# Issuing the fourth and fifth image pairs' loads from another place in a dilated 3x3 convolution

## The chip, the cores and the metric

The kernel runs on one core of a Trainium2 chip. A core has a matrix engine (TensorE, PE in the profile), a vector engine (VectorE, DVE), a scalar engine (ScalarE, ACT), GpSimd (POOL), a synchronisation engine (SyncE, SP) that here only issues transfers, and 16 DMA engines that move data between the device memory (HBM) and the on-chip memory (SBUF). TensorE writes its results to a separate accumulator memory (PSUM). The metric is the device time of one execution in microseconds; 13 executions of the kernel before have a median of 128.17 us, from 127.54 to 131.16.

## The reference

A 3x3 convolution with dilation 2 and zero padding 2, in float32: 16 images of 64 channels, 64 x 64 pixels, to 128 channels.

```python
batch, c_in, h, w, c_out, k, dilation = 16, 64, 64, 64, 128, 3, 2
...
x_pad = np.pad(x, ((0, 0), (0, 0), (pad, pad), (pad, pad)), mode='constant')
...
                    output[b, co] += weight[co, ci, kh, kw] * x_pad[b, ci, kh*dilation:kh*dilation+h, kw*dilation:kw*dilation+w]
```

The input is 16.8 MB, the output 33.6 MB, the weights 0.3 MB.

## The kernel before

**Tiling.** Two images share the 128 partitions: one pair's input is a tile of 128 partitions (two images times 64 channels) by 4096 pixels in float32, 2 MB, and there are 8 pairs. Each pair is worked off in four groups of 16 rows, so the main loop (L196) runs over 32 groups, G = 0 to 31. One pair's output is 128 channels by 2 x 4096 pixels, 4 MB.

**What a group does.** The rows are paired two apart, so that part of the products is shared: VectorE adds row blocks (`rowsum`, L85, into `xs`), TensorE forms the shared product psP from `xs` and two further products psA and psB from the casted input (all matmuls are at L174), ScalarE copies psP from PSUM to SBUF (`p_sb`, L230), and VectorE adds it to psA and to psB into the output tile `osb` (L237). There is only one PSUM buffer for psP (`ppool`, bufs=1), so the next group's psP waits for the copy.

**Input.** `load` (L61) fetches one pair's float32 input into one of three buffers (`fpool`, bufs=3). ScalarE casts it to float16 in four chunks per pair (`cast`, L73); casts are numbered c = 0 to 31. `casts(G)` (L153) is called in each group behind the copy of psP (in group 0 ahead of it) and runs up to two casts, up to seven casts ahead of the group for the first two pairs, up to three ahead later. When a pair's last cast has been issued, that pair's float32 buffer is free, and the same function issues the load of the pair three later into it (L162).

**Queues.** SyncE issues the weights (L88), the first pair's load in two pieces (L89) and the second and third pair's loads (L90, L91), and after that only stores (L188). All later loads (fourth to eighth pair) are issued by ScalarE, between its casts and copies. Every transfer is split over the same 16 DMA engines; in the profile q1 holds what SyncE issued and q10 what ScalarE issued. The stores of a pair, one per image, are issued when its fourth group is done (L253, L254); the last pair's are cut into smaller pieces.

**Order.** The schedule is written by hand: each engine runs its instructions in the order of the program, and waits where data isn't there.

Of the kernel before, what the change touches and what calls it, by code (L numbers as in the profile page):

```python
# [10 lines left out]
def kernel(  # L11
# [7 lines left out]
    nc = tc.nc  # L19

    B, CI, H, W = x.shape
# [15 lines left out]
    NG = H // GR  # L37
# [5 lines left out]
    XF = 3  # L43
# [17 lines left out]
    def load(pb, cuts=(0, H), queue=nc.sync):  # L61
        x32_tiles[pb] = fpool.tile([P, HW], f32, tag="x32", name="x32")
        for lo, hi in zip(cuts[:-1], cuts[1:]):
            queue.dma_start(  # L64
                out=x32_tiles[pb][:, lo * W : hi * W], in_=x_pair[pb, :, lo * W : hi * W]
            )

    def cast(c):
        pb, g = divmod(c, NG)
        lo, hi = chunk_rows[g]  # L70
        if g == 0:
            x16_tiles[pb] = xpool.tile([P, HW], f16, tag="x16", name="x16")
        nc.scalar.copy(  # L73
            out=x16_tiles[pb][:, lo * W : hi * W], in_=x32_tiles[pb][:, lo * W : hi * W]
        )

    def rowsum(c):
        pb, g = divmod(c, NG)
        if g == 0:
            xs_tiles[pb] = sxpool.tile([P, HW // 2], f16, tag="xs", name="xs")  # L80
        v = x16_tiles[pb][:, g * GR * W : (g + 1) * GR * W].rearrange(
            "p (b e q) -> p b e q", e=2, q=2 * W
        )
        s = xs_tiles[pb][:, g * NH : (g + 1) * NH].rearrange("p (b q) -> p b q", q=2 * W)
        nc.vector.tensor_tensor(out=s, in0=v[:, :, 0], in1=v[:, :, 1], op=add)  # L85
# [67 lines left out]
    def casts(G):  # L153
        for n in range(2 if G else 3):
            c = ahead[0]
            if c >= ngroups or c > G + (7 if c < 2 * NG else 3):
                return
            cast(c)
            ahead[0] += 1
            if c % NG == NG - 1 and c // NG + XF < npairs:  # L160
                k = c // NG + XF
                load(k, (0, H) if k < 6 else (0, H // 2, H), queue=nc.scalar)  # L162

    def product(ps, src, kind, blk0, nblk, first, last):
        for j in (1, 0, 2):
            dw = (j - 1) * d
            o0, o1 = max(0, -dw), W - max(0, dw)
            t = kind * KW + j
            for hb in range(2):
                pp = slice(hb * CI, (hb + 1) * CI)  # L170
                rhs = src(pp, dw + o0, dw + o1)
                po = ps[:, hb * NH + blk0 * 2 * W : hb * NH + (blk0 + nblk) * 2 * W]
                po = po.rearrange("p (r w) -> p r w", w=W)[:, :, o0:o1]
                nc.tensor.matmul(  # L174
                    out=po,
                    lhsT=w_sb[pp, t * CO : (t + 1) * CO],
                    rhs=rhs,
                    start=first and j == 1,
                    stop=last and j == 2,
                )  # L180

    def blocks(x16, b0, n, e):
        v = x16.rearrange("p (b e r w) -> p b e r w", e=2, r=2, w=W)
        return lambda pp, c0, c1: v[pp, b0 : b0 + n, e, :, c0:c1]

    def store(pb, m, r0=0, r1=H, rows=((0, P),)):
        for lo, hi in rows:
            nc.sync.dma_start(  # L188
                out=out_img[2 * pb + m, lo:hi, r0 * W : r1 * W],
                in_=o_tiles[pb][lo:hi, m * HW + r0 * W : m * HW + r1 * W],  # L190
            )
# [4 lines left out]
    for G in range(ngroups):  # L196
        pb, g = divmod(G, NG)
        x16 = x16_tiles[pb]
        xs = xs_tiles[pb].rearrange("p (r w) -> p r w", w=W)
        if g == 0:  # L200
            o_tiles[pb] = opool.tile([P, 2 * HW], f32, tag="osb", name="osb")
        o = o_tiles[pb].rearrange("p (m b e q) -> p m b e q", m=2, e=2, q=2 * W)
        b0 = g * NBLK

        def summed():
            ps = ppool.tile([P, 2 * NH], f32, tag="p", name="psP")
            sv = lambda pp, c0, c1: xs[pp, g * GR // 2 : (g + 1) * GR // 2, c0:c1]
            product(ps, sv, 0, 0, NBLK, True, True)
            return ps

        if G:
            psP = summed()

        psA = apool.tile([P, 2 * NH], f32, tag="ab", name="psA")
        product(psA, blocks(x16, b0, NBLK, 1), 1, 0, NBLK, True, False)
        z = 1 if g == 0 else 0
        product(psA, blocks(x16, b0 + z - 1, NBLK - z, 1), 2, z, NBLK - z, False, True)

        psB = apool.tile([P, 2 * NH], f32, tag="ab", name="psB")
        product(psB, blocks(x16, b0, NBLK, 0), 3, 0, NBLK, True, False)  # L220
        z = 1 if g == NG - 1 else 0
        product(psB, blocks(x16, b0 + 1, NBLK - z, 0), 4, 0, NBLK - z, False, True)

        if not G:
            psP = summed()

        if not G:
            casts(0)
        p_sb = spool.tile([P, 2 * NH], f32, tag="psb", name="p_sb")
        nc.scalar.copy(out=p_sb, in_=psP)  # L230
        if G:
            casts(G)
        if G + 1 < ngroups:
            rowsum(G + 1)
        pv = p_sb.rearrange("p (m b q) -> p m b q", m=2, q=2 * W)
        for e, ps in ((0, psA), (1, psB)):
            nc.vector.tensor_tensor(  # L237
                out=o[:, :, b0 : b0 + NBLK, e],
                in0=ps.rearrange("p (m b q) -> p m b q", m=2, q=2 * W),
                in1=pv,  # L240
                op=add,
            )

        if pb == npairs - 1:
            if g % 2 == 1:
                store(pb, 0, (g - 1) * GR, (g + 1) * GR)
                if g == NG - 1:
                    store(pb, 1, (g - 1) * GR, H - ROWS4)
                    store(pb, 1, H - ROWS4, H, FOUR)
                else:  # L250
                    store(pb, 1, (g - 1) * GR, (g + 1) * GR)
        elif g == NG - 1:
            store(pb, 0)  # L253
            store(pb, 1)  # L254
# [37 lines left out]
```

## Time and profile before

| | us |
|---|---|
| median of 13 runs | 128.17 |
| lowest and highest run | 127.54, 131.16 |
| the profiled execution | 127.58 |
| its span, from the first to the last instruction | 125.7 |
| PE busy, share of the span | 104.7 (83%) |
| DVE busy, share of the span | 90.8 (72%) |
| ACT busy, share of the span | 65.0 (52%) |
| bytes moved by DMA, mean rate | 50.78 MB, 404 GB/s |
| issue of the fourth, fifth and sixth pairs' loads | 10.88, 19.21, 36.87 |
| issue of the first pair's stores | 23.28 and 23.67 |

The profile's page gives busy time by engine, then the span in 40 equal slices of 3.14 us (a digit is the busy share in tenths, 9 meaning 90% or more), then groups of instructions, and a chain of waits followed back from the last instruction. Other views of the same trace give the chain in order of time, a table of chosen stretches, the timeline of one engine, and the DMA queues in a stretch. All times are counted from the first instruction. Names like `psP` or `x` stand for all buffers of that name; "ACTq" and "SPq" are the two engines' instructions that issue transfers.

### The profile page before, as it was taken

How to read it: one execution, taken by the hardware profiler on the slowest of the kernel's cores; microseconds unless marked ns; L12 is line 12 of the kernel's file. 1: busy time of each engine (PE TensorE's matmuls, PEld its weight loads, DVE VectorE, ACT ScalarE, POOL GpSimd, SP SyncE). 2: the span in 40 equal slices, each digit the busy share in tenths (PEclk: the TensorE clock that was granted, in tenths of full speed). 3: DMA queues.
4: the chain of work that ended last, by engine and by line, in shares of the span. 5: the costliest groups of instructions: out<-in, count | busy, mean ns of one | idle time of the engine just before them, and what ended most of it. 6: DMA issues, size and time to landing. Idle time of an engine off the chain costs nothing.

```text
span 125.7 us, 2335 instructions
## 1 busy us (share of the span) xinstructions
PE 104.7 (83%) x1000; PEld 56.7 (45%) x1000; DVE 90.8 (72%) x103; ACT 65.0 (52%) x68; POOL 2.2 (2%) x8
## 2 busy tenths in 40 slices
PE   6884999999999999999999999999999999500000
PEld 2351555555555555555555555555555555200000
DVE  0660998988898889798969898889888988700000
ACT  4377794366656665666566666666666633100000
POOL 2400000000000000000000000000000000000000
PEclk9999999999999999999999999999999999965555
DMA  4999999999999999999999999999999999999971
GB/s 109 391 434 448 438 427 422 427 302 433 427 433 433 427 417 433 417 443 417 409 448 407 433 433 417 433 420 427 433 448 422 427 417 427 427 417 427 424 325 54
DMA packets 4466, 50.78 MB, mean 404 GB/s; under 512 B 488, under 2 KB 488, under 8 KB 1000
## 3 DMA queue, kind: packets, MB, share of 16 engines
q1 hardware_dynamic: 3448, 40.14, 75.7%
q10 hardware_dynamic: 1008, 10.49, 20.5%
q8 instruction: 8, 0.13, 0.4%
q14 instruction: 2, 0.02, 0.0%
HBM read 17.07 MB, written 33.55 MB: 403 GB/s over the span
## 4 chain that ended last, share of the span: by engine, by line
PE 76%; DMA 6%; ACT 2%; issue 1%; DVE 1%; DVEq 1%; SPq 1%; ACTq 0%
PE psA L174 30%; PE psB L174 29%; PE psP L174 16%; DMA x<-in_x_dram 6%; DVE osb L237 1%; DVEq L287 1%; ACT p_sb L230 1%; ACT x L73 1%; SPq L64 0%; SPq L88 0%; ACTq L64 0%; DVEq L237 0%
## 5 line engine op out<-in xcount | busy, mean ns | idle before, releaser
L174 PEld LDWEIGHTS <-w_sb 64*128 64x128 f16 x960 | 54.6, 94 | 46.8 <-issue 2.1
L230 ACT COPY p_sb<-psP 128x1024 f32<-128x1024 f32 x32 | 32.4, 1012 | 37.5 <-PE psP L174 18.0
L237 DVE TENSOR_TENSOR osb<-psA,p_sb 128x1024 f32<-128x1024 f32 x32 | 39.2, 1225 | 14.2 <-PE psA L174 8.4
L174 PE MATMUL psA<-x,w_sb 64*128 64x496 f16 (+3 forms) x384 | 45.1, 365 | 0.3 <-ACT x L146 0.3
L174 PE MATMUL psB<-x,w_sb 64*128 64x496 f16 (+3 forms) x384 | 45.1, 365 | 0.0
L237 DVE TENSOR_TENSOR osb<-psB,p_sb 128x1024 f32<-128x1024 f32 x32 | 39.1, 1221 | 0.0
L73 ACT CAST x<-x 128x1024 f16<-128x1024 f32 (+2 forms) x31 | 32.1, 1044 | 0.4 <-DMA x<-in_x_dram 0.4
L174 PE MATMUL psP<-xs,w_sb 64*128 64x496 f16 (+1 forms) x192 | 26.0, 371 | 1.8 <-ACT p_sb L230 1.8
L85 DVE TENSOR_TENSOR xs<-x 128x512 f16<-128x512 f16 x32 | 13.3, 416 | 0.7 <-ACT x L73 0.7
L101 PE MATMUL dm<-zero 128*128 128x512 f16 x10 | 4.1, 532 | 1.2 <-DVE zero L93 1.2
L111 DVE CAST wd<-w 128x192 f16<-128x192 f32 x1 | 0.5, 505 | 2.7 <-DMA w<-in_weight_dram 2.7
L101 PEld LDWEIGHTS <-zero 128*128 128x128 f16 x10 | 1.0, 120 | 2.6 <-issue 1.3
L124 PE MATMUL wt<-ident,wd 128*64 128x128 f16 x30 | 1.6, 241 | 0.5 <-DVE wd L111 0.5
L124 PEld LDWEIGHTS <-wd 128*64 128x64 f16 x30 | 1.0, 118 | 2.0 <-DVE wd L111 1.4
L113 ACT ACT_TABLE_LOAD x1 | 1.3, 1283 | 0.7 <-PEq L273 0.7
L113 ACT CAST wd<-w 128x192 f16<-128x192 f32 x1 | 0.5, 542 | 1.8 <-DMA w<-in_weight_dram 1.8
L136 ACT CAST w_sb<-wt 128x384 f16<-128x384 f32 x1 | 0.5, 478 | 1.4 <-PE wt L124 1.4
L93 DVE MEMSET zero<- 128x256 uint32 x1 | 0.3, 272 | 0.9 <-PEq L273 0.9
L138 DVE CAST w_sb<-wt 128x384 f16<-128x384 f32 x1 | 0.6, 558 | 0.4 <-PE wt L124 0.4
L112 POOL TENSOR_TENSOR wd<-w 128x192 f16<-128x192 f32 x1 | 0.8, 797 | 2.6 <-DMA w<-in_weight_dram 2.6
L146 ACT CAST x<-x 128x512 f16<-128x512 f32 x1 | 0.6, 618 | 0.4 <-DMA x<-in_x_dram 0.4
L115 POOL CAST wd<-w 128x192 f16<-128x192 f32 x1 | 0.8, 807 | 0.0
(11 smaller groups left out, 3.8 us busy)
## 6 DMA issues: line engine op xcount, KB each, us to landing
out_dram<-osb SPq DMA_DIRECT2D x14, 2048.0 KB, 17.3
x<-in_x_dram ACTq DMA_DIRECT2D x3, 2048.0 KB, 14.6
x<-in_x_dram SPq DMA_DIRECT2D x2, 2048.0 KB, 16.6
x<-in_x_dram ACTq DMA_DIRECT2D x4, 1024.0 KB, 15.6
out_dram<-osb SPq DMA_DIRECT2D x3, 1024.0 KB, 14.2
x<-in_x_dram SPq DMA_DIRECT2D x1, 1088.0 KB, 5.5
x<-in_x_dram SPq DMA_DIRECT2D x1, 960.0 KB, 7.3
out_dram<-osb SPq DMA_DIRECT2D x1, 704.0 KB, 14.1
```

Source lines behind the costliest of these rows:

```text
L73: nc.scalar.copy(out=x16_tiles[pb][:, lo * W : hi * W], in_=x32_tiles[pb][:, lo * W : hi * W])
L85: nc.vector.tensor_tensor(out=s, in0=v[:, :, 0], in1=v[:, :, 1], op=add)
L101: nc.tensor.matmul(out=dm[:, 0:512], lhsT=zero[:, 0:P], rhs=zero)
L112: nc.gpsimd.tensor_tensor(out=wdv[:, 3], in0=wv[:, 0], in1=wv[:, 1], op=sub)
L113: nc.scalar.copy(out=wdv[:, 2], in_=wv[:, 0])
L115: nc.gpsimd.tensor_copy(out=wdv[:, 4], in_=wv[:, 2])
L124: nc.tensor.matmul(out=wts[k % 3][r * CI : (r + 1) * CI, c0 + j * CO : c0 + (j + 1) * CO], lhsT=wd[:, t * CI : (t + 1) * CI], rhs=ident,)
L138: nc.vector.tensor_copy(out=t2[0], in_=t2[1])
L174: nc.tensor.matmul(out=po, lhsT=w_sb[pp, t * CO : (t + 1) * CO], rhs=rhs, start=first and j == 1, stop=last and j == 2,)
L230: nc.scalar.copy(out=p_sb, in_=psP)
L237: nc.vector.tensor_tensor(out=o[:, :, b0 : b0 + NBLK, e], in0=ps.rearrange("p (m b q) -> p m b q", m=2, q=2 * W), in1=pv, op=add,)
L287: with _tile.TileContext(nc) as tc:
```

## The change

The fourth pair's load (k = 3) stays at the same place in the program, after the last cast of the first pair in group 0, but is issued by SyncE (the default of `load`) in place of ScalarE. So it stands in SyncE's order between the third pair's load and the first pair's stores. The fifth pair's load (k = 4) is no longer issued after the last cast of the second pair, which is in group 2, but by ScalarE in group 6, after that group's cast. The later loads stay where they were.

```diff
@@ -159,7 +159,10 @@
             ahead[0] += 1
             if c % NG == NG - 1 and c // NG + XF < npairs:
                 k = c // NG + XF
-                load(k, (0, H) if k < 6 else (0, H // 2, H), queue=nc.scalar)
+                if k == XF:
+                    load(k)
+                elif k > XF + 1:
+                    load(k, (0, H) if k < 6 else (0, H // 2, H), queue=nc.scalar)
@@ -230,6 +233,8 @@
         nc.scalar.copy(out=p_sb, in_=psP)
         if G:
             casts(G)
+        if G == NG + 2:
+            load(XF + 1, queue=nc.scalar)
         if G + 1 < ngroups:
             rowsum(G + 1)
```

## The prediction

> **What bounds the kernel now.** I read the page first: the totals and the 40 slices.
>
> ```profile
> span 125.7 us, 2335 instructions
> PE 104.7 (83%) x1000; PEld 56.7 (45%) x1000; DVE 90.8 (72%) x103; ACT 65.0 (52%) x68; POOL 2.2 (2%) x8
> ...
> PE   6884999999999999999999999999999999500000
> ...
> DMA  4999999999999999999999999999999999999971
> GB/s 109 391 434 448 438 427 422 427 302 433 427 433 433 427 417 433 417 443 417 409 448 407 433 433 417 433 420 427 433 448 422 427 417 427 427 417 427 424 325 54
> ```
>
> TensorE is full from slice 5 on, but it stops some 15 us before the end, while the DMA row stays at 9 to the 38th slice. So the DMA engines are the bound, and TensorE is a second resource not far below it. The rate is flat at about 430 GB/s except at the start, at the end and in the ninth slice (25.1 to 28.3 us), where it is 302 although the engines are counted as busy.
>
> The second view is the chain of waits in order of time, for the start and the end.
>
> ```profile
> 9.92 0.94 ACT x L73
> 10.86 0.02 issue
> 10.88 0.38 ACTq L64
> 11.26 0.04 issue
> 11.30 1.02 ACT p_sb L230
> 12.33 0.04 issue
> 12.37 0.81 PE psP L174 x6
> ...
> 107.49 1.23 DVE osb L237
> 108.71 1.13 DVEq L287
> ```
>
> The chain follows compute alone: ScalarE's last cast of pair 0, the issue of the fourth pair's load, the first copy of psP, then TensorE without a break. That chain ends at 109.8; behind it only transfers run. The table by stretches and the timeline of SyncE's queue show it (engine columns, then granted clock, DMA share and GB/s):
>
> ```profile
> 0.00:1.70 1.70, 0.51 (x2) 0.24 (x3) 0.27 (x1) 0.97 (x1) 0.70 (x6) 1.00 0.00 0
> 0.00:23.00 23.00, 19.19 (x173) 9.60 (x175) 14.38 (x20) 14.38 (x17) 2.25 (x8) 1.00 0.94 383
> 1.70:5.00 3.30, 2.85 (x13) 0.90 (x12) 1.18 (x3) 0.86 (x2) 1.13 (x2) 1.00 0.97 311
> 25.00:28.20 3.20, 3.20 (x34) 1.74 (x32) 2.78 (x4) 2.06 (x2) 0.00 (x0) 1.00 0.98 307
> 83.00:96.00 13.00, 13.00 (x132) 7.24 (x128) 11.60 (x13) 8.23 (x9) 0.00 (x0) 1.00 1.01 429
> 109.90:120.00 10.10, 0.00 (x0) 0.00 (x0) 0.00 (x0) 0.00 (x0) 0.00 (x0) 0.54 1.00 423
> ```
>
> ```profile
> 0.74 0.40 SPq L88 DMA_DIRECT2D w<-in_weight_dram  x1
> ...
> 23.28 0.82 SPq L188 DMA_DIRECT2D out_dram<-osb  x2
> ...
> 109.87 3.55 SPq L188 DMA_DIRECT2D out_dram<-osb  x4
> ```
>
> After the last add 423 GB/s flow for another 10.1 us, about 4.3 MB of stores that had piled up. A later TensorE costs nothing as long as it is less than some 10 us later; every microsecond in which the DMA engines stand still before 120 us is paid in full. Undisturbed rate: 429 GB/s (row 83 to 96).
>
> The low slice belongs to the first store. Its issue is at 23.28; the DMA view from 23.3 to 26.8 shows what moved since:
>
> ```profile
> q10 hardware_dynamic: 82, 1.33, 104.3%
> q1 hardware_dynamic: 1, 0.00, 0.0%
> ```
>
> q1 is SyncE's queue (stores), q10 ScalarE's (here the fifth pair's load). For 3.5 us the store moves no row; only load rows pass, and from 25 us on more slowly. The stretch 25.0 to 28.2 moves 307 instead of 429: (429 - 307) / 429 x 3.2 = 0.91 us of DMA time is lost. That is what the change can win at most.
>
> **The change part by part.**
>
> *What is removed from ScalarE's start.* The issue of the fourth pair's load costs 0.38 us plus 0.04 (11.30 - 10.88 = 0.42) on the chain ahead of the first copy of psP. SyncE issues it now, behind the third pair's load; SyncE then waits for the last cast of pair 0 (10.86), and behind that wait only the first store is queued, which isn't due before 22.9. So TensorE, the adds and the first store come 0.42 earlier: the store is issued at 23.28 - 0.42 = 22.86. At the end this is worth nothing, because the 10 us backlog of stores hides it; without that backlog it would be a gain of 0.42.
>
> *The fourth pair's load in SyncE's queue.* Same 2 MB, same engines, now behind the third pair's load instead of beside it. Its data is first needed by the cast in group 9, at 38.9; cost 0. The second and third pairs' data come sooner, which nothing waits for (TensorE has no gap there).
>
> *The fifth pair's load moved.* It was issued at 19.21; now it follows the cast of group 6, which ends at 30.76, so about 30.4 with the shift. Its 0.34 us on ScalarE fits into the idle time before the next copy (1.22 us there; without that it would delay one copy by 0.34, hidden again by the backlog). Its data is needed by the cast at 51.8; even behind 4 MB of stores and shared with the sixth pair's load it lands by about 45. The sixth pair's load stays at 36.87 and queues behind it; it is needed at about 64. Cost 0 on the compute side.
>
> *What this does to the DMA engines.* This is the sum. Weights and four pairs are 288 + 1088 + 960 + 3 x 2048 KB = 8.68 MB. By 23.0 us the engines had been given 383 x 23.0 = 8.81 MB; a row of 16 KB is booked when it starts and 16 engines are on average half way through theirs (0.13 MB), so 8.68 MB are done at 23.0. In the old kernel the fifth pair's load is queued behind them. In the new one there is nothing, until the first store flows. How long does a DMA take from its issue to its first bytes on idle engines? The trace has one: the weights, issued at 0.74, no bytes before 1.70, bytes in the next 0.2 us, so 1.05 us. First store bytes at 22.86 + 1.05 = 23.91. Gap: 23.91 - 23.0 = 0.91 us, on all engines but a late one. Bounds: 0 (if the loads drain up to a microsecond later than the mean) and 22.86 + 3.5 - 23.0 = 3.4 (if the store takes the 3.5 us that it takes today behind full queues). I take 0.91, since the queue is empty then and the weights' row is the one for an empty queue.
>
> *What the first store itself costs.* The 0.91 us lost from 25.0 to 28.2 are no longer lost on loads. Whether the store still pays them on itself no row shows directly. Bounds: 0 (it was the mixing with loads) and 0.91 (it is the start of a store). The nearest row is the other start from an empty queue, that of the loads: 1.70 to 5.00 moves 311, (429 - 311) / 429 x 3.3 = 0.91 us lost with no store about. And mixing alone is not slow later: from slice 14 on loads and stores share the engines at about 425. So I take the full 0.91.
>
> Sum: gap +0.91, old loss -0.91, new loss +0.91: +0.91 us. Next stretch: pair 0's stores (4.2 MB, 9.8 us) then last from 23.9 to about 34.6; the fifth pair's load is queued from 30.4, the second pair's stores from 35.2, so no second gap. From there each pair brings 6.3 MB, 14.7 us of DMA, against 12.4 us of TensorE: saturated again to the end.
>
> Weighed against the Trainium skill: its page "DMA: Bandwidth & Descriptors", section "Latency and other measured facts", gives about 600 ns to the first byte for queues of this kind, where the trace has 1.05; by the page the gap would be 0.46 and the sum an estimated +0.46, no change that can be told. The same page, "Back-pressure in remote DMA", says that stalled writes hold up the other queues of their engine; it speaks of traffic between cores, and no run here shows the mechanism. It speaks against the change: the store's stall would remain when the loads are gone, and the sum would be the +0.91.
>
> The profiled execution took 127.58 (span 125.7 and 1.9 around it), the median of the runs is 128.17, 0.59 above. New profiled execution: 128.49; new median: 129.08, so 129.1.
>
> **The rivals.** (B) *No change:* the first store runs at full rate once it is alone, and its gap eats the gain: +0.91 - 0.91 = 0, 128.2. For it: the low stretch ends as soon as store rows flow. Against it: the slow start of the loads with nothing beside them.
>
> (C) *Faster:* no gap and no slow start. It decides if the engines still hold load rows when the store's first bytes are ready, that is, if the four loads end 0.9 us later than 23.0 or the store starts 0.9 earlier. Sum -0.91: 127.3. For it: the issue is at 22.86, before the drain, and the engines don't all drain at once. Against it: 1.05 us is the only latency on idle engines in the trace, and ending the loads later costs as much as it fills.
>
> (D) *Much slower:* the store needs 3.5 us from issue to bytes even on idle engines. Gap 3.4, sum +2.5 to +3.4: 130.6 to 131.5. For it: both transfers that I can see start that late (the fourth pair's load, issued at 10.88, too moves nothing until 14.3). Against it: engines were full in both cases, and the weights took 1.05.
>
> That the change doesn't do what it says is unlikely: SyncE and ScalarE each carry the load in the place named, and neither waits for anything late there. What can fail is "empty load queue" as a benefit, which is case B or A.
>
> **How the numbers follow.** A (slower by 0.91 and its bounds of 0.4 to 1.4) 0.47; B 0.32; C 0.16; D 0.05. A measurement of this kernel can tell about 0.5% (0.64 us) from no change: below 127.53 is faster, above 128.81 slower. Of A 0.38 lies above and 0.09 within; of B 0.28 within and 0.02 on either side; of C 0.15 below and 0.01 within; D is slower. Faster 0.17, same 0.38, slower 0.45. Range 127.4 to 130.2: it takes in A and B and reaches into C; left out are a good half of C and D. A's own range is 128.5 to 129.6.
>
> **What would show it.** In the new profile: a slice at about 23 us with the DMA share well below 9 (the gap, 0.9 us); q1 rows from about 23.9; the rate from 24 to 27 below 429 by about 0.9 us of DMA time (A) or not (B); no dip at 25 to 28 on load rows; the first copy of psP at about 10.9; no TensorE gap after 12; the rest of the GB/s row as before, with the end 0.9 later. Wrong is the prediction if the engines never stand still near 23 us, if the gap is beyond 2 us, or if TensorE or an add waits for a load in groups 9 to 20.

## The result and the profile after

The changed kernel is slower: 129.28 us median of 11 runs (128.83 to 130.96) against 128.02 us of 48 runs of the kernel before; the ratio is 1.012, 95% interval 1.0086 to 1.0154. Two repeats of the comparison gave 1.0157 (1.0104 to 1.021) and 1.0164 (1.0101 to 1.0227). All ratios are taken over the fast executions alone, those within 1.5% of the fastest of their kernel, so they differ a little from the ratio of the medians.

The changed kernel was profiled three times. Its first execution took 130.96 us; this is its page: busy time, the busy tenths and the rate in 40 slices of 3.23 us.

```profile
span 129.2 us, 2335 instructions
...
PE   6898799999999999999999999999999999000000
...
DMA  5999999299999999999999999999999999999971
GB/s 139 376 454 426 436 426 426 91 406 467 309 431 284 441 416 416 436 419 429 439 431 429 416 439 421 419 441 436 411 446 426 411 436 446 406 413 426 427 316 56
```

The third execution took 129.29 us, near the median. The same lines of its page (slices of 3.19 us):

```profile
span 127.5 us, 2335 instructions
...
PE   6975999999999999999999999999999999000000
...
DMA  4999999699999999999999999999999999999971
GB/s 131 374 462 427 421 427 442 288 411 468 319 375 339 432 432 427 419 414 439 416 432 432 429 424 434 411 447 432 421 416 442 437 421 416 432 424 419 424 315 58
```

Both have a slice in which the DMA row falls (the eighth: 2 and 6), the forecast gap, and then, with the DMA row at 9, two more slow places, which were not forecast: slices 11 to 13 (319, 375, 339 in the second fence). The slow place of the old kernel, 302 in the ninth slice, is gone from there. The third trace stands below for the changed kernel, because TensorE starts in it as it did in the profile before; in the first and second it started late (see the last section).

The gap, in the table by stretches of the third trace (engine columns, granted clock, DMA share, GB/s) and in the timeline of SyncE's queue:

```profile
22.50:23.50 1.00, 1.00 (x14) 0.62 (x12) 0.83 (x3) 0.79 (x1) 0.00 (x0) 1.00 0.12 49
...
30.00:36.00 6.00, 6.00 (x64) 3.35 (x61) 5.41 (x7) 3.73 (x5) 0.00 (x0) 1.00 0.98 366
36.00:42.00 6.00, 6.00 (x60) 3.19 (x58) 5.30 (x6) 3.77 (x5) 0.00 (x0) 1.00 1.00 355
42.00:83.00 41.00, 41.00 (x402) 22.33 (x398) 36.01 (x40) 26.12 (x27) 0.00 (x0) 1.00 1.01 428
```

```profile
11.10 0.33 SPq L64 DMA_DIRECT2D x<-in_x_dram  x1
22.94 0.82 SPq L191 DMA_DIRECT2D out_dram<-osb  x2
```

The engines stand still around 23 us while the first store has only just been issued. The stretches 30 to 36 and 36 to 42 move 366 and 355 at full DMA share; the kernel before moved 426 and 434 there. After 42 the two kernels are alike (428 and 425 from 42 to 83). The same stretches of the kernel before:

```profile
30.00:36.00 6.00, 6.00 (x62) 3.42 (x60) 5.44 (x6) 3.73 (x5) 0.00 (x0) 1.00 1.00 426
36.00:42.00 6.00, 6.00 (x61) 3.22 (x58) 5.46 (x6) 3.77 (x4) 0.00 (x0) 1.00 1.02 434
42.00:83.00 41.00, 41.00 (x400) 22.66 (x398) 35.68 (x41) 26.11 (x28) 0.00 (x0) 1.00 1.01 425
```

To put figures on it, I spread each transfer row's bytes evenly over its time in the trace and counted what is missing to 430 GB/s; such figures are called *lost* below. Lost, in us of DMA time:

| | first store issued | gap at 23 | next 6 us | where loads join stores | where stores join loads | span |
|---|---|---|---|---|---|---|
| before | 23.28 | none | | 0.06 (30 to 45) | 0.88 (22 to 30) | 125.7 |
| changed, third trace | 22.94 | 0.91 | 0.08 | 0.75 (30.5 to 36) | 1.07 (36 to 45) | 127.5 |
| changed, first trace | 24.60 | 2.52 | 0.07 | 0.81 | 1.01 | 129.2 |

Third trace against before: 0.91 + 0.08 + 0.75 + 1.07 - 0.06 - 0.88 = 1.9 us; the span grew by 1.8. First trace against before: 3.5 us lost, and the span grew by 3.5.

### The profile page after: what moved, and what is told of

Same layout as the page of the kernel before. It is cut to its first block, busy times and chain, and to the rows that moved or that the text cites. A ratio compares the mean times of both kernels' runs of the same rounds, so it can differ in the third digit from the quotient of the medians.

```text
span 129.2 us, 2335 instructions
## 1 busy us (share of the span) xinstructions
PE 107.1 (83%) x1000; PEld 57.2 (44%) x1000; DVE 90.7 (70%) x103; ACT 64.9 (50%) x68; POOL 2.2 (2%) x8
## 4 chain that ended last, share of the span: by engine, by line
PE 80%; DMA 2%; DVE 1%; DVEq 1%; ACT 1%; issue 0%
PE psA L177 31%; PE psB L177 30%; PE psP L177 16%; DMA w<-in_weight_dram 2%; PE wt L124 2%; PE dm L101 2%; DVE osb L242 1%; DVEq L292 1%; ACT p_sb L233 1%; DVE wd L111 0%; DVEq L242 0%
## 5 line engine op out<-in xcount | busy, mean ns | idle before, releaser
L177 PE MATMUL psA<-x,w_sb 64*128 64x496 f16 (+3 forms) x384 | 46.1, 371 | 0.0
L101 PE MATMUL dm<-zero 128*128 128x512 f16 x10 | 5.0, 623 | 1.2 <-DVE zero L93 1.2
L124 PEld LDWEIGHTS <-wd 128*64 128x64 f16 x30 | 1.5, 162 | 2.5 <-DVE wd L111 1.3
L124 PE MATMUL wt<-ident,wd 128*64 128x128 f16 x30 | 2.2, 314 | 0.4 <-DVE wd L111 0.4
L138 DVE CAST w_sb<-wt 128x384 f16<-128x384 f32 x1 | 0.6, 558 | 1.2 <-PE wt L124 1.2
L148 DVE CAST w_sb<-wt 128x384 f16<-128x384 f32 x1 | 0.6, 557 | 0.4 <-PE wt L124 0.4
## 6 DMA issues: line engine op xcount, KB each, us to landing
out_dram<-osb SPq DMA_DIRECT2D x14, 2048.0 KB, 18.9
```

The lines of the kernel that those rows point to most:

```text
L101: nc.tensor.matmul(out=dm[:, 0:512], lhsT=zero[:, 0:P], rhs=zero)
L124: nc.tensor.matmul(out=wts[k % 3][r * CI : (r + 1) * CI, c0 + j * CO : c0 + (j + 1) * CO], lhsT=wd[:, t * CI : (t + 1) * CI], rhs=ident,)
L138: nc.vector.tensor_copy(out=t2[0], in_=t2[1])
L177: nc.tensor.matmul(out=po, lhsT=w_sb[pp, t * CO : (t + 1) * CO], rhs=rhs, start=first and j == 1, stop=last and j == 2,)
```

## The experiments

After the first trace I held two theories. One was of queues: the loss arises where one transfer's last rows meet the first rows of another queue. The other was the forecast itself, that it belongs to the first store; against it, the first store had lost almost nothing at its own start (0.07).

**1 and 2. The same two kernels again.** No edit.

> The changed kernel once more, for a second trace of it. In its first trace the DMA engines stand still for about 2.5 us (23 to 25.5 us), because TensorE ran its first group late and the first store was issued at 24.6 instead of the 22.9 that I forecast. Theory 1 (a gap plus losses where one queue takes over from the other): with the first store at 22.9 the gap is 0.9 to 1.1 us, the store then flows at 420 to 430 GB/s at once, and two slow stretches follow, at about 33 to 35 and 39 to 41 us, of 0.8 to 1.0 us each; time 129.0 to 129.3. Theory 2 (the slow start belongs to the first store, as predicted): 0.9 us lost in the first 3 us of the store, no loss at 33 to 41; same time.

> The kernel before once more. If the slow stretch at 25 to 28 us is a part of this schedule, it is there again at the same place with 0.8 to 1.0 us lost, and nowhere else. If it is a chance event of one execution, it is absent or elsewhere, and the two slow stretches of the changed kernel lose their weight as evidence too. Time 127.6 to 128.2.

The changed kernel had a late TensorE again: first store at 24.75, gap 2.78, then 0.07, 0.81 and 1.02 lost, 131.06 us. The forecast of the gap's length for 22.9 was not tested by it; the two later losses came at the same places. The kernel before lost 1.05 from 22 to 30 and 0.08 from 30 to 45 (128.47 us). So the slow places belong to the schedules. In its runs this second copy of the kernel before came out at a ratio of 1.0034 (1.0003 to 1.0064) to the kernel before: a difference of some 0.3% between two kernels says nothing here.

**3. Both loads on SyncE.** The edit is shown against the changed kernel.

```diff
-                if k == XF:
+                if k <= XF + 1:
                     load(k)
-                elif k > XF + 1:
+                else:
...
-        if G == NG + 2:
-            load(XF + 1, queue=nc.scalar)
```

> Fourth and fifth pair's loads both issued by SyncE ahead of the first store: load rows last until about 27.9, the first store stands behind them in the same queue, so there is neither a gap nor a second queue beside it. Theory 1 (loss only where one queue's last rows meet the first rows of the other): no slow stretch at 25 to 28, the next meeting is the sixth pair's load beside a long row of stores at 40, which cost nothing before; 0.9 us less than the kernel before, ratio 0.993. Theory 2 (the first store costs 0.9 us wherever it starts among loads): slow stretch at the hand-over stays, ratio 1.000.

Measured: ratio 1.0008 (0.9969 to 1.0046). In its table by stretches:

```profile
20.00:25.00 5.00, 5.00 (x54) 2.88 (x52) 4.41 (x6) 1.35 (x2) 0.00 (x0) 1.00 0.99 426
25.00:30.00 5.00, 5.00 (x52) 2.67 (x48) 4.17 (x6) 3.54 (x4) 0.00 (x0) 1.00 1.01 360
```

No gap, but 0.84 lost from 22 to 30 although the stores stand behind the loads in one queue. A meeting of two queues isn't needed, and that form of the theory falls.

**4. The first part of the change alone,** and once more for a narrower interval (10). The edit is shown against the kernel before.

```diff
-                load(k, (0, H) if k < 6 else (0, H // 2, H), queue=nc.scalar)
+                if k == XF:
+                    load(k)
+                else:
+                    load(k, (0, H) if k < 6 else (0, H // 2, H), queue=nc.scalar)
```

> Only the first part of the change: the fourth pair's load on SyncE, the fifth pair's issued by ScalarE in group 2 as before. Both theories: no gap, since the fifth pair's load covers 23 to 28 us; the slow stretch when the first store meets the last rows of the fifth pair's load stays, about 0.9 us; ratio 1.000. If the first part alone costs something, ratio above 1.004, the gap is not the cause of the loss.

> The first part of the change alone once more, for a narrower interval: 0.4 us less on ScalarE ahead of the first copy of psP, which the backlog of stores hides at the end. By the reading that DMA time alone counts the ratio is 1.000; if the earlier first store is worth its 0.4 us, 0.997.

Ratios 0.9969 (0.9937 to 1.0001) and 1.0018 (0.9985 to 1.0051); no gap; 0.84 lost from 22 to 30 in the first trace and 1.00 in the second, whose TensorE was late (first store at 24.57). The first part alone costs nothing, and the 0.4 us on ScalarE earn nothing that can be told. From the first trace's table by stretches:

```profile
20.00:25.00 5.00, 5.00 (x54) 2.86 (x52) 4.42 (x6) 1.30 (x2) 0.00 (x0) 1.00 1.02 433
25.00:30.00 5.00, 5.00 (x50) 2.66 (x48) 4.17 (x6) 3.69 (x4) 0.00 (x0) 1.00 0.99 357
```

**5. The second part alone,** against the kernel before.

```diff
                 k = c // NG + XF
-                load(k, (0, H) if k < 6 else (0, H // 2, H), queue=nc.scalar)
+                if k == XF:
+                    load(k, queue=nc.scalar)
+                elif k > XF + 1:
+                    load(k, (0, H) if k < 6 else (0, H // 2, H), queue=nc.scalar)
...
+        if G == NG + 2:
+            load(XF + 1, queue=nc.scalar)
```

> Only the second part of the change: the fourth pair's load is issued by ScalarE in group 0 as before, the fifth pair's in group 6. If the loss comes from the later load of the fifth pair alone, this has the gap and both later losses of the changed kernel; the first store is issued 0.4 us later (23.3), so the gap is 1.3 in place of 0.9: ratio 1.012 to 1.016. If the fourth pair's load in SyncE's queue is needed for the loss, ratio below 1.004.

Ratio 1.0175 (1.0122 to 1.0228), from four executions. Its table by stretches (first store issued at 24.05, TensorE late):

```profile
22.00:25.00 3.00, 3.00 (x34) 1.80 (x32) 2.83 (x4) 1.01 (x1) 0.00 (x0) 1.00 0.41 175
...
31.00:36.00 5.00, 5.00 (x52) 2.77 (x50) 4.58 (x5) 2.73 (x4) 0.00 (x0) 1.00 1.02 367
...
38.00:42.00 4.00, 4.00 (x42) 2.12 (x38) 3.58 (x5) 2.16 (x3) 0.00 (x0) 1.00 0.97 311
```

Gap (2.02) and both later losses (0.82 and 1.01) are there. The gap is longer than the forecast 1.3 because the first store was issued 0.75 us later than expected. The whole loss comes from moving the fifth pair's load.

**6. Pair 0's stores in halves, in the kernel before.** By then I had two new theories: H, that a transfer of the other direction costs if few rows are left when it is issued, and D, that each change from loads alone to loads and stores costs.

```diff
+        elif pb == 0:
+            if g % 2 == 1:
+                store(pb, 0, (g - 1) * GR, (g + 1) * GR)
+                store(pb, 1, (g - 1) * GR, (g + 1) * GR)
         elif g == NG - 1:
```

> The kernel before, with pair 0's stores cut in halves: the first halves are issued after group 1, at about 17.3, when each DMA engine still has 9 load rows of 16 KB before it, more than in any of the five losses seen so far (6 to 8 rows left at the issue of a transfer of the other direction). Theory H (the loss arises where a transfer of the other direction is issued with 8 rows or fewer left): no slow stretch from 17 to 30; 0.8 us less, ratio 0.993. Theory D (each change from loads alone to loads and stores costs 0.8 to 1.0, however many rows are left): a slow stretch at about 19 to 22, none at 25 to 28; ratio 1.000.

Ratio 0.9979 (0.9929 to 1.003). In its table by stretches the slow place has moved forward with the store, to 20 to 23, and 25 to 28 is clean:

```profile
18.00:20.00 2.00, 2.00 (x23) 1.07 (x20) 2.00 (x2) 1.54 (x3) 0.00 (x0) 1.00 0.99 426
20.00:23.00 3.00, 3.00 (x34) 1.69 (x32) 2.58 (x4) 1.08 (x2) 0.00 (x0) 1.00 0.97 344
23.00:30.00 7.00, 7.00 (x71) 3.82 (x69) 6.27 (x8) 3.85 (x5) 0.00 (x0) 1.00 1.00 421
```

0.56 lost from 18 to 25, less than D's 0.8 to 1.0: for D, against H, though 9 rows are close to H's 8.

**7 and 8. The fifth pair's load in group 4 or 5.** The edit against the changed kernel for group 5 (experiment 8); for group 4 (experiment 7) the line reads `if G == NG:`.

```diff
-        if G == NG + 2:
+        if G == NG + 1:
```

> The changed kernel with the fifth pair's load issued in group 4 in place of 6, at about 23.2, right behind the first store: both meet idle engines. All theories: the gap at 23 us stays (0.9 us with the first store at 22.9, up to 2.6 if TensorE starts late). If the two later losses (33 to 35 and 39 to 41) come from the fifth pair's load and the second pair's stores each meeting a nearly finished transfer, the first is gone, and the second depends on the rows left at 35.2 (about 5: Theory H has a loss at 38, Theory D has none, since loads have ended by then). Ratio by D about 1.001, by H 1.007.

> The changed kernel with the fifth pair's load issued in group 5, at about 27.2 (or 29 with a late TensorE), when 10 to 11 store rows are left on each engine in place of 8. Theory H: the loss at 33 to 35 is gone. Theory D (the first mixing of stores and loads costs 0.8 whatever is left): it comes at 31 to 33. Both: the gap stays. Ratio by H 1.004 to 1.006, by D 1.010.

Group 5: ratio 1.0068 (1.0024 to 1.0113). The load was issued at 25.16, earlier than I had expected, with some 13 store rows left on each engine, and still 0.87 was lost where it joined (28 to 33). H falls; the ratio alone would not have told, as its interval holds both forecasts. But the loss at 39 to 41 is gone:

```profile
22.00:24.00 2.00, 2.00 (x23) 1.13 (x20) 1.83 (x3) 1.01 (x1) 0.00 (x0) 1.00 0.65 279
24.00:28.00 4.00, 4.00 (x40) 2.15 (x38) 3.58 (x5) 2.06 (x2) 0.00 (x0) 1.00 1.05 442
28.00:31.00 3.00, 3.00 (x31) 1.60 (x29) 2.58 (x4) 1.96 (x2) 0.00 (x0) 1.00 0.93 284
31.00:45.00 14.00, 14.00 (x138) 7.68 (x136) 12.28 (x14) 9.05 (x10) 0.00 (x0) 1.00 1.02 428
```

Group 4: ratio 1.004 (0.9991 to 1.0089), which holds D's 1.001 and H's 1.007. TensorE was late in its trace (129.69 us; the median is 128.44), and the load did not go out behind the first store, but 0.64 us ahead of it:

```profile
23.53 0.38 ACTq L64 DMA_DIRECT2D x<-in_x_dram  x1
24.17 0.82 SPq L191 DMA_DIRECT2D out_dram<-osb  x2
```

```profile
24.50:28.50 4.00, 4.00 (x42) 2.13 (x38) 3.44 (x4) 2.04 (x3) 0.00 (x0) 1.00 1.05 315
28.50:31.00 2.50, 2.50 (x28) 1.32 (x24) 2.08 (x4) 1.35 (x3) 0.00 (x0) 1.00 0.89 367
```

The DMA view from 24.5 to 28.5 has load rows alone:

```profile
q10 hardware_dynamic: 77, 1.26, 104.6%
```

The load's first row is at 24.58, the first store row at 28.88, 4.7 us after the store's issue. So the two did not start together: once more a store joined loads that ran alone. 1.92 were lost to 25.0 and 1.33 from 25 to 31, then 0.07 from 31 to 45; H's loss at 38 did not come. The losses of this trace can't be parted into that of the load's own start on idle engines and that of the store behind it.

**9. The changed kernel a third time.** No edit.

> The changed kernel a third time, for a trace in which TensorE's first group isn't late. The length of the gap should follow the issue of the first store: issue + 0.95 - 23.0, as it did in the other traces with a gap (24.60 gave 2.5, 24.05 gave 2.0, 22.76 gave 0.7). With an issue at 22.8 to 22.9: gap 0.7 to 0.9, time 128.9 to 129.3; with a late start (24.6): gap 2.5, time 130.6 to 131. The losses where the fifth pair's load joins the stores and where the second pair's stores join the loads are there in both cases, 0.8 and 1.0.

First store at 22.94, gap 0.91, then 0.08, 0.75 and 1.07, 129.29 us: as expected (22.94 + 0.95 - 23.0 = 0.89).

**11. Halves and the first part together.** Pair 0's stores as in 6, the fourth pair's load as in 4.

> The fourth pair's load on SyncE, the fifth pair's in group 2 as in the kernel before, and pair 0's stores in halves. No gap, one change from loads alone to loads and stores, at about 20 to 22, which cost 0.5 with half stores in place of 0.85 with whole ones: ratio 0.994 to 0.998. If neither part is worth anything in the end, 1.000.

Ratio 1.0013 (0.9977 to 1.0049). TensorE was late in its trace, and 1.28 were lost from 18 to 26 where I had expected 0.5; the forecast gain of 0.2 to 0.6% did not come. No version tried is faster than the kernel before by more than its interval.

## Why the prediction was right, and where it wasn't

The time, 129.1 forecast and 129.28 measured, and the direction were right. The mechanism was right in one half, and luck had a hand in how close the time came. The forecast for the profiled execution was 128.49, 0.91 above 127.58; the third one, with TensorE in time as before, took 129.29, so 0.80 was missing. The forecast of the median added 0.59, the distance of the old median from the old profiled execution; the median of the changed kernel, 129.28, has no such distance from 129.29. The two errors nearly cancel.

**The gap: right, to size.** Forecast 0.91 us with the first store issued at 22.86; measured 0.91 with 22.94. Its terms held: the four loads were done at about 23.0, and store rows began some 0.85 us after the issue (24.60 to 25.45 in the first trace; I had taken 1.05 from the weights, a load, and a load on idle engines took 1.05 again in experiment 7, from 23.53 to 24.58). Over five traces it follows the issue of the first store: lost 0.72, 0.91, 2.02, 2.52 and 2.78 for 22.76, 22.94, 24.05, 24.60 and 24.75. The prediction called itself wrong if the gap was beyond 2 us, and in two of the changed kernel's three traces it was (2.52 and 2.78): not because a store takes longer to start, but because the first store was issued 1.7 and 1.9 us later than forecast, a delay of TensorE that the prediction did not have. Rival D's 3.5 us on idle engines is refuted, and so is rival C: the engines did stand still. The 600 ns to the first byte that the Trainium skill gives ("DMA: Bandwidth & Descriptors", "Latency and other measured facts") are 0.25 below the measured 0.85; my 1.05 was 0.20 above it.

**ScalarE's start: right.** The chain in order of time of the third trace shows the copy of psP directly behind the casts, with no issue between them:

```profile
9.19 1.88 ACT x L73 x2
11.07 0.92 ACT p_sb L233
11.99 0.04 issue
12.03 0.81 PE psP L177 x6
```

TensorE goes on at 12.03 in place of 12.37. As forecast this is worth nothing at the end (experiment 4).

**The first store's own loss: this is the step that failed.** The prediction said "So I take the full 0.91", by the likeness to the loads' start. In all traces in which the first store met idle engines alone, it lost 0.03 to 0.08 in its first 3.5 to 6 us. Rival B's half of the argument was right here. The row taken as likeness was no like case either. In its first 0.8 us (1.7 to 2.5) only the weights moved, in 42 rows of about 2.3 KB where the later loads and the stores have rows of 16 KB:

```profile
DMA packets 42, 0.10 MB, mean 121 GB/s; under 512 B 0, under 2 KB 0, under 8 KB 42
```

At 121 in place of 429 that is 0.57 of the 0.91 us. How loads of long rows start on idle engines with nothing issued beside them, no run here shows.

**"No second gap": this failed as well, in the other direction.** The prediction let the engines run at 429 whenever something was queued. They were never idle again, but lost 0.75 and 1.07. The DMA view of the third trace from 37 to 39 shows what stands behind the second:

```profile
q10 hardware_dynamic: 37, 0.61, 112.1%
q1 hardware_dynamic: 1, 0.00, 0.0%
```

Pair 0's stores had ended, the second pair's were issued at 35.3 but not yet moving, and the delayed loads ran alone. So the old slow place, a change from loads alone to loads and stores, was made once more at 39, and the first mixing of the two directions, which no schedule tried here avoids, came at 32 to 34. The forecast sum was gap 0.91 - 0.91 + 0.91; the measured one is 0.91 - 0.88 + 0.75 + 1.07 = 1.85 in this trace. My single term of +0.91 stood in for two that come to 1.82, so the forecast was about half of what the trace shows, while the medians differ by 1.3 in the first comparison and by 1.8 and 1.9 in the repeats.

**What is shown and what is not.** Shown: the loss comes from moving the fifth pair's load (5 against 4); it does not need two queues (3) nor a nearly finished transfer (8); the place moves with the store (6); keeping stores beside the loads removes the second loss (8). Stores that joined loads running alone lost 0.56 to 1.28 in every trace where they did so (in that of experiment 7, with the load's own start, more). Loads that joined stores lost 0.75 to 0.87 the first time, but only 0.05 to 0.08 at about 40 us in the kernel before, in 3 and in the first trace of 4; with a late TensorE (10 and 11) it was 0.47 and 0.26. Why the first mixing costs and the later one hardly does is open, and so is what in the DMA engines makes a change of direction slow; no run here looks inside them.

## What to carry to other kernels

When the DMA engines are the bound, as here, a transfer that is early is cover: delaying it can't win more than the slow stretch that it seems to cause (0.9 us here), and it opens a gap until the next transfer's first rows (0.9 us here, 2.8 with a late TensorE). Before a schedule is changed to avoid a slow meeting of loads and stores, check by moving the meeting whether it goes away or only comes elsewhere. In this kernel it paid to keep both directions queued together rather than in turns: that is what removed the 1.07 us in experiment 8.

## What had not been expected of the hardware

**TensorE's start varies from run to run, and the gap exposes it.** The small matmuls of the weights (L124) and the first psA, in the first and then in the third trace of the changed kernel (start, length, count):

```profile
7.04 0.85 PE L124 MATMUL wt<-ident,wd 128*64 128x128 f16 x12
...
8.37 2.31 PE L177 MATMUL psA<-x,w_sb 64*128 64x512 f16 x12
```

```profile
5.98 0.53 PE L124 MATMUL wt<-ident,wd 128*64 128x128 f16 x12
...
7.55 1.29 PE L177 MATMUL psA<-x,w_sb 64*128 64x512 f16 x12 [0.72 <-ACT x L146]
```

(In brackets: idle time before it, and what ended it.) The same instructions take 1.6 to 1.8 times as long in the first trace, until about 10.5 us, with the granted clock recorded as 1.00 in both. The first store is issued 1.66 us later for it. The changed kernel pays this in full: 129.29 us against 130.96 and 131.06. With the fifth pair's load early (experiment 4) the same delay, first store at 24.57 in place of 22.86, cost 127.41 against 128.36, about half. The Trainium skill ("TensorE: Matmul & The Clock Gate", "What you observe") has the array go from half to full rate about 4 us into sustained matmuls; matmuls start at 1.19 here, so the third trace agrees (six of its 128x128 matmuls take 0.53 us at 4.16, twelve take 0.53 at 5.21) and the first, with full rate only after some 9 us, does not. The matmuls pause once before 4.6 us, but the pause does not tell the traces apart: it is 0.37 and 0.67 us in the two late ones, 0.23 in the third, and 0.45 in the kernel before, which started in time.

**An issue can overtake the instruction ahead of it.** The fifth pair's load stands behind group 6's cast in ScalarE's order, but went out at 28.51 in the third trace, before that cast began (29.38):

```profile
28.51 0.37 ACTq L64 DMA_DIRECT2D x<-in_x_dram  x1
29.38 1.05 ACT L73 CAST x<-x 128x1024 f16<-128x1024 f32 x1
```

It had nothing to wait for there: the last cast from its buffer is one of group 2, which ended at 18.9. Forecast was 30.4. In experiment 8 it went out at 25.16 in place of 27.2 in the same way, and in experiment 7 at 23.53, ahead of the first store.
